# A decoder trunk on one core: the second FFN products of two phases as seven block products, their sums returned through device memory

## The chip, the core and the metric

The kernel runs on one core of a Trainium2 chip. The time is that of one execution on the device in microseconds, as the median of three runs. The engines are named as the profile names them: PE multiplies matrices, PEld loads its weights, DVE and ACT work on elements, POOL starts the software DMAs and does some element work, SP starts the hardware DMAs. All DMA queues of the core use the same 16 DMA engines.

## The reference

Two layers, each a mixer and a feed-forward network (FFN), on x of 512 positions by 1024 in float32. The mixer of layer 0 joins a gated linear recurrence and retention, that of layer 1 is a sparse attention; the change touches neither. The FFN's hidden width is 2816.

```python
def swiglu(x, w1, w3, w2):
    return (jax.nn.silu(x @ w1) * (x @ w3)) @ w2

def reference(x, ...):
    h = x
    for layer in range(DEPTH):
        ...
        h = h + swiglu(rmsnorm(h, ffn_norm[layer]), ffn_w1[layer], ffn_w3[layer], ffn_w2[layer])
    return rmsnorm(h, final_norm)
```

## The kernel before

**Precision.** Every float32 matrix product is made of three matmuls: an operand is split into a high part (`hi`, a copy in a rounded type, ACT, L136 for weights) and what is left (`lo`, a subtraction, DVE, L137), and `mm3` (L201 to L203) adds hi by hi, lo by hi and hi by lo in one PSUM bank.

**Residual stream.** `h` lies transposed in two tiles, feature by position, so a sum that comes out position by feature has to be turned on PE before it can be added.

**Phases.** `ffn` goes through the hidden width in three phases, `ph` 0 and 1 of 1024 and 2 of 768. A phase has two sets (`q` 0 and 1), each of them a call of `strassen`: the products of x with a 512 (384) wide piece of w1 and of w3 in one, as a 2 by 2 block product that takes seven block products instead of eight. These are, in order, A11, A12, S1, S4, S2, S3 and A22, named by their left operand; each is 2 halves of the positions by 4 blocks of the depth by 3 matmuls, 24. They add up in the PSUM banks X, Y, V, V, X, X and Z. Between them `keep` copies a bank away (ACT, L286) and `add` adds a bank to what was kept (DVE, L290), both with the norm's factor for a position. X is used three times over: the kept X of A11, then S2 on top, read for the block 12, then S3 on top, read for the block 22.

**Gating and turning.** `after` (L732) multiplies silu of the one by the other (L741), and `turn` transposes the result on PE (L726) to g, feature by position, in high part `gh` (L729) and low part `gl` (L730).

**Second products.** At the end of each phase g goes through w2 as plain products: 8 tiles of the output, each 8 (6) blocks of depth by 3 matmuls, so 192 for 1024; `done` (L767) adds a tile's PSUM bank to h.

**Weights.** `plan` and `plan_set` list the loads ahead. A plain unit is 1 MB by SP (L117), of two parts of 1024 columns. A set loads three of its four weight blocks by SP and makes the sums that the seven products want in place, by eight accumulating DMAs by POOL (L161): each may only start when DVE has split what stood there. It has 14 parts. Raw weights, high parts and low parts have four buffers each, and splits run three parts ahead of PE. A framework sets the order of each engine from the program's order and priorities; every engine then works in order.

Of the kernel before, what the change touches and what calls it, by code (L numbers as in the profile page):

```python
# [17 lines left out]
F32 = mybir.dt.float32  # L18
F32R = mybir.dt.float32r
# [5 lines left out]
P = 128  # L25
# [38 lines left out]
class Trunk:  # L64
# [210 lines left out]
    def strassen(self, sg, n, after, last):  # L275
# [8 lines left out]
        def keep(b, name, i, r):  # L284
            c = rest[name, i] = self.g2([P, S], name="part")[:, 0:n]
            A.activation(c, ps[b, i][:, 0:n], AF.Copy, scale=r())  # L286

        def add(b, name, i, r):
            c = rest.pop((name, i))
            V.scalar_tensor_tensor(c, ps[b, i][:, 0:n], r(), c, op0=ALU.mult, op1=ALU.add)  # L290
            after(name, i, c)
        R = lambda t: (lambda: self.rtok[:, t:t + 1])
        N = lambda t: (lambda: self.ntok[:, t:t + 1])
        for j, (b, op) in enumerate((("X", "A11"), ("Y", "A12"), ("V", "S1"), ("V", "S4"), ("X", "S2"), ("X", "S3"), ("Z", "A22"))):
            last(j)
            if j == 1:
                for i in range(2):
                    keep("X", "11", i, R(i))
            first = j in (0, 1, 2, 6)
            for i in range(2):  # L300
                if first:
                    ps[b, i] = self.psA("ps_" + b) if b in "XV" else self.psB("ps_" + b)
                o = ps[b, i][:, 0:n]
                self.mm3(o, [self.sg_at(sg, op, p, slice(i * P, (i + 1) * P)) + w.at((j * 4 + p) * n, (j * 4 + p + 1) * n) for p in range(4)], first, True, j in (3, 4, 5))
                if j == 1:
                    add("Y", "11", i, R(i))
                elif j == 2:
                    keep("V", "22", i, R(2 + i))
                elif j == 3:
                    keep("V", "12", i, R(i))  # L310
                elif j == 4:
                    add("X", "12", i, N(i))
                elif j == 5:
                    add("X", "22", i, N(2 + i))
# [369 lines left out]
    def plan_ffn(self, layer):  # L684
        for ph in range(3):
            for j in range(2):
                if ph < 2:
                    self.plan_set("wff%d" % layer, (2 * ph + j,), 2048)
                else:
                    self.plan_set("wfg%d" % layer, (j,), 1536)  # L690
            for j in range(2):
                if ph < 2:
                    self.plan("w2a%d" % layer, 2 * ph + j, 2048)
                else:
                    self.plan("w2b%d" % layer, j, 1536)
            for j in range(2):
                if ph < 2:
                    self.plan("w2c%d" % layer, 2 * ph + j, 2048)
                else:
                    self.plan("w2d%d" % layer, j, 1536, 768)  # L700

    def ffn(self, layer, sg, gain_next, want_hg=True):
# [10 lines left out]

        for ph in range(3):
            gs = []
            for q in range(2):
                n = S if ph < 2 else 3 * P
                nj = n // P
                g = [self.b8([P, 4, S], F32R, name="g" + x) for x in "hl"]
# [3 lines left out]
                def turn(t, v, g=g, nj=nj):  # L723
# [3 lines left out]
                    p4 = pt[:, 0:nj * P].rearrange("p (j c) -> p j c", j=nj)  # L727
                    hi, lo = (x[:, 0:nj, t * P:(t + 1) * P] for x in g)
# [24 lines left out]
                self.strassen(sg, n, after, before)  # L753
# [20 lines left out]
            flush(7)  # L774
            w = [self.unit(), self.unit()]
# [36 lines left out]
        return hn  # L812

# [559 lines left out]
def pack(i):  # L1373
# [28 lines left out]
    for l in range(2):  # L1402
# [8 lines left out]
        o["w2a%d" % l] = c(np.stack([w2u((4 * q, 4 * q + 4), (0, 4)) for q in range(4)]))  # L1411
        o["w2b%d" % l] = c(np.stack([w2u((16 + 3 * q, 19 + 3 * q), (0, 4)) for q in range(2)]))
        o["w2c%d" % l] = c(np.stack([w2u((8 * ph, 8 * ph + 8), (4 + 2 * q, 6 + 2 * q)) for ph in range(2) for q in range(2)]))
# [28 lines left out]
```

## Time and profile before

| | us |
|---|---|
| median of 3 runs | 1243.75 |
| the three runs | 1243.32 to 1243.83 |
| the profiled execution | 1243.25 |
| its span, first to last instruction | 1241.3 |
| PE busy | 1221.3 (98%) |
| DVE busy | 797.6 (64%) |
| ACT busy | 684.3 (55%) |
| POOL busy | 230.8 (19%) |

The span has 1.95 us less than the execution's time. The FFN of layer 0 lies at about 215 to 557 us, that of layer 1 at about 887 to 1235 us. A busy share says how long an engine had work, not whether anybody waited for it; that is seen in waits and in the chain that ended last.

### The profile page before, as it was taken

How to read it: one execution, taken by the hardware profiler on the slowest of the kernel's cores; microseconds unless marked ns; L12 is line 12 of the kernel's file. 1: busy time of each engine (PE TensorE's matmuls, PEld its weight loads, DVE VectorE, ACT ScalarE, POOL GpSimd, SP SyncE). 2: the span in 40 equal slices, each digit the busy share in tenths (PEclk: the TensorE clock that was granted, in tenths of full speed). 3: DMA queues.
4: the chain of work that ended last, by engine and by line, in shares of the span. 5: the costliest groups of instructions: out<-in, count | busy, mean ns of one | idle time of the engine just before them, and what ended most of it. 6: DMA issues, size and time to landing. Idle time of an engine off the chain costs nothing.

```text
span 1241.3 us, 16441 instructions
## 1 busy us (share of the span) xinstructions
PE 1221.3 (98%) x6077; PEld 1030.5 (83%) x6077; DVE 797.6 (64%) x1237; ACT 684.3 (55%) x1395; POOL 230.8 (19%) x303
## 2 busy tenths in 40 slices
PE   9999999999999999999999999999999999999997
PEld 8788888888888889987888878877888888889996
DVE  6886639666356636775264889985976546653664
ACT  6541447664256426655454688995766336633653
POOL 0001420220012002100000567681111011101200
PEclk9999999999999999999999999999999999999999
DMA  9221143784378428852100000124588358825832
GB/s 343 69 102 68 35 169 102 174 187 150 101 182 184 133 69 178 222 201 77 68 35 1 1 1 1 35 96 171 130 182 200 107 124 185 200 81 107 181 90 68
DMA packets 35535, 149.23 MB, mean 120 GB/s; under 512 B 3936, under 2 KB 6256, under 8 KB 26624
## 3 DMA queue, kind: packets, MB, share of 16 engines
q1 hardware_dynamic: 21296, 100.88, 22.7%
q0 software_dynamic: 14016, 47.27, 21.4%
q8 instruction: 48, 0.79, 0.3%
q14 instruction: 31, 0.25, 0.1%
q10 hardware_dynamic: 144, 0.04, 0.0%
HBM read 143.98 MB, written 4.19 MB: 119 GB/s over the span
## 4 chain that ended last, share of the span: by engine, by line
PE 87%; ACT 5%; DVE 4%; issue 1%; POOL 1%; DMA 0%; POOLq 0%; DVEq 0%; SPq 0%; ACTq 0%
PE ps L203 6%; PE ps L201 6%; PE ps L202 6%; PE ps_t L201 5%; PE ps_t L203 5%; PE ps_t L202 5%; PE ps_X L201 5%; PE ps_X L203 5%; PE ps_X L202 5%; PE ps_V L201 3%; PE ps_V L203 3%; PE ps_V L202 3%; ACT prob L1184 2%; PE ps_Y L201 2%; PE ps_Z L201 2%; PE ps_Z L203 2%
## 5 line engine op out<-in xcount | busy, mean ns | idle before, releaser
L136 ACT CAST whi<-wr 128x512 fp32r<-128x512 f32 (+1 forms) x540 | 294.9, 593 | 347.2 <-PE ps L202 126.0
L137 DVE TENSOR_TENSOR wlo<-wr,whi 128x1024 fp32r<-128x1024 f32 (+2 forms) x272 | 313.4, 1154 | 209.1 <-ACT whi L136 201.9
L201 PE MATMUL ps<-gh,whi 128*128 128x512 f32 (+1 forms) x364 | 139.8, 384 | 0.0
L203 PE MATMUL ps<-gh,wlo 128*128 128x512 f32 (+1 forms) x364 | 139.2, 382 | 0.0
L202 PE MATMUL ps<-gl,whi 128*128 128x512 f32 (+1 forms) x364 | 139.1, 382 | 0.0
L161 POOL DMA_DIRECT2D wr<-wff x64 | 55.5, 866 | 376.1 <-DVE wlo L137 329.4
L201 PE MATMUL ps_t<-whi,hgh 128*128 128x512 f32 x288 | 114.7, 399 | 0.0
L202 PE MATMUL ps_t<-wlo,hgh 128*128 128x512 f32 x288 | 113.4, 394 | 0.0
L203 PE MATMUL ps_t<-whi,hgl 128*128 128x512 f32 x288 | 112.7, 391 | 0.0
L201 PE MATMUL ps_X<-whi,sg 128*128 128x512 f32 (+1 forms) x288 | 107.1, 372 | 0.4 <-DVE part L290 0.3
L203 PE MATMUL ps_X<-whi,sg 128*128 128x512 f32 (+1 forms) x288 | 106.9, 371 | 0.0
L202 PE MATMUL ps_X<-wlo,sg 128*128 128x512 f32 (+1 forms) x288 | 106.8, 371 | 0.0
L1194 POOL TENSOR_TENSOR prob<-prob,rs 128x384 f32<-128x384 f32 (+3 forms) x128 | 88.0, 721 | 1.9
L767 DVE TENSOR_TENSOR h<-ps,h 128x512 f32<-128x512 f32 x46 | 31.8, 691 | 82.5 <-PE ps L203 82.5
L203 PEld LDWEIGHTS ps<-gh,wlo 128*128 128x128 f32 x364 | 68.4, 188 | 13.4
L202 PEld LDWEIGHTS ps<-gl,whi 128*128 128x128 f32 x364 | 68.4, 188 | 13.1
L201 PEld LDWEIGHTS ps<-gh,whi 128*128 128x128 f32 x364 | 68.4, 188 | 12.9
L1184 ACT ACTIVATE prob<-ps_s,nm 128x384 f32<-128x384 f32 (+3 forms) x128 | 68.1, 540 | 15.8 <-DVE nm L1180 15.0
L201 PE MATMUL ps_V<-whi,sg 128*128 128x512 f32 (+1 forms) x192 | 71.4, 372 | 0.0
L203 PE MATMUL ps_V<-whi,sg 128*128 128x512 f32 (+1 forms) x192 | 71.2, 371 | 0.0
L202 PE MATMUL ps_V<-wlo,sg 128*128 128x512 f32 (+1 forms) x192 | 71.2, 371 | 0.0
L203 PEld LDWEIGHTS ps_t<-whi,hgl 128*128 128x128 f32 x288 | 54.1, 188 | 11.5 <-issue 0.2
(316 smaller groups left out, 2565.2 us busy)
## 6 DMA issues: line engine op xcount, KB each, us to landing
wr<-wff POOLq DMA_DIRECT2D x64, 512.0 KB, 5.7
wr<-wff SPq DMA_DIRECT2D x24, 1024.0 KB, 4.8
wr<-wfg POOLq DMA_DIRECT2D x32, 384.0 KB, 5.8
wr<-w0t SPq DMA_DIRECT2D x10, 1024.0 KB, 6.0
wr<-w1t SPq DMA_DIRECT2D x10, 1024.0 KB, 4.9
wr<-wfg SPq DMA_DIRECT2D x12, 768.0 KB, 4.4
wr<-w2a SPq DMA_DIRECT2D x8, 1024.0 KB, 4.8
wr<-w2c SPq DMA_DIRECT2D x8, 1024.0 KB, 4.9
```

The costliest lines, as they stand in the source:

```text
L136: self.nc.scalar.copy(hi[:, c], x[:, c])
L137: self.nc.vector.tensor_tensor(lo, x, hi.bitcast(F32), op=ALU.subtract)
L161: self.nc.gpsimd.dma_start(x[:, c], more[:, c], accum_op=ALU.add)
L201: mm(ps, ah, bh, start=(first and k == 0), stop=False)
L202: mm(ps, ah, bl, start=False, stop=False)
L203: mm(ps, al, bh, start=False, stop=(last and k == n - 1))
L767: V.tensor_tensor(hm, ps, hm, op=ALU.add)
L1184: A.activation(u.p[:, r, b, 0:u.nk], u.ps[:, b, :], AF.Exp, bias=u.nm[:, b:b + 1], accum_out=u.rs[:, r, b:b + 1])
L1194: Q.tensor_tensor(x, x, u.rs[:, r, b:b + 1].broadcast_to([P, u.nk]), op=ALU.mult)
```

## The change

In phases 0 and 1 the second products are a `strassen` call too, on new weights `w2s` (three loads and eight accumulations of 512 KB, 14 parts) in place of `w2a` and `w2c` (four plain loads, 8 parts). `second` makes the six operands from g (`make`: ACT high, DVE low, in halves, two operand tiles `gop` in flight) and their sums (`sums1`, `sums2`, DVE). `turn` leaves g as it comes in these phases. The results come out position by feature. They are not added to h but stored in device memory (`sums`, 8 stores a phase by SP). In the last phase, step by step (a step is one block product, 14 in the phase), SP loads the eight tiles of phase 0's sums into the operand buffers of that phase (`back`), POOL adds those of phase 1 to them by accumulating DMAs one step later, and three products behind that `turned` transposes them (4 transposes a tile) and adds them to h. The last phase's own products stay as they were. `keep` and `add` have a form without factor; the sign is in the operation.

```diff
-    def strassen(self, sg, n, after, last):
+    def strassen(self, opnd, n, after, last, scaled=True):
...
+            if scaled:
+                A.activation(c, ps[b, i][:, 0:n], AF.Copy, scale=r())
+            else:
+                with self.tc.high_priority(offset=20):
+                    A.copy(c, ps[b, i][:, 0:n])
...
+                V.tensor_tensor(c, c, ps[b, i][:, 0:n], op=ALU.subtract if sub else ALU.add)
...
+            if ph < 2:
+                self.plan_set("w2s%d" % layer, (ph,), 2048)
+                continue
...
+        sums = self.dram.tile([2, NT, P, D], F32, name="sums%d" % layer)
+        back = []
+
+        def turned(t, c, tiles):
+
+            pt = self.psC("ps_tr")
+            for k in range(4):
+                T.transpose(pt[:, k * P:(k + 1) * P], tiles[:, k * P:(k + 1) * P], self.ident)
+            x = h[c][:, :, t * P:(t + 1) * P]
+            V.tensor_tensor(x, pt.rearrange("p (k s) -> p k s", k=4), x, op=ALU.add)
+
...
+                    if nj == 4:
+                        A.copy(g[:, :, t * P:(t + 1) * P], p4)
+                        return
...
+                    if ph == 2:
+
+                        step = 7 * q + j
+                        for i in range(8):
+                            src = [sums[u, i // 2, :, i % 2 * S:(i % 2 + 1) * S] for u in range(2)]
+                            if step == i + 2:
+                                if i % 4 == 0:
+                                    back.append(self.b8([P, 4, S], name="back"))
+                                nc.sync.dma_start(back[i // 4][:, i % 4], src[0])
+                            elif step == i + 3:
+                                nc.gpsimd.dma_start(back[i // 4][:, i % 4], src[1], accum_op=ALU.add)
+                            elif step == i + 6:
+                                turned(i // 2, i % 2, back[i // 4][:, i % 4])
...
+            if ph < 2:
+                self.second(gs[0][0], gs[1][0], sums[ph], flush)
+                continue
...
+    def second(self, g0, g1, dst, flush):
...
+        def make(n):
+            t = ops[n] = self.b8([P, 2, 4, 256], F32R, name="gop")
+            for c in (slice(0, 2), slice(2, 4)):
+                x = src[n][0 if c.start == 0 else 1] if n == "S1" else src[n][:, c]
+                with self.tc.high_priority(offset=16):
+                    A.copy(t[:, 0, c], x)
+                    V.tensor_tensor(t[:, 1, c], x, t[:, 0, c].bitcast(F32), op=ALU.subtract)
...
+        def before(j):
+            while stores:
+                self.nc.sync.dma_start(*stores.pop(0))
+            if j == 0:
+                make("A12")
+            elif j == 1:
+                flush(99)
+                sums1()
+                make("S1")
+                sums2()
+            elif j < 6:
+                make(("S4", "S2", "S3", "A22")[j - 2])
+
+        def after(name, i, c):
+            t = 2 * (name[0] == "2") + i
+            u = name[1] == "2"
+            stores.append((dst[t, :, u * S:(u + 1) * S], c))
+
+        make("A11")
+        self.strassen(lambda n, p, c: tuple(ops[n][:, z, p, c] for z in range(2)), S, after, before, False)
+        before(7)
```

The order of DVE in the middle of the second product of layer 0's phase 0, before: splits of weights (`wlo`) by turns with adds of a finished bank to h.

```order
L767 TENSOR_TENSOR h_1434<-ps_2_2482,h_1434 128x512
L137 TENSOR_TENSOR wlo_2623<-wr_2384,whi_2622 128x1024
L767 TENSOR_TENSOR h_1435<-ps_2_2621,h_1435 128x512
L137 TENSOR_TENSOR wlo_2656<-wr_2443,whi_2655 128x1024
L767 TENSOR_TENSOR h_1435<-ps_2_2652,h_1435 128x512
L137 TENSOR_TENSOR wlo_2688<-wr_2443,whi_2687 128x1024
```

The same engine at the fifth and sixth product there, after. L866 makes the low part of an operand `gop` (here S3's in the first row and A22's in the fourth), L298 is the new `add`; banks `ps_X_2482` and `ps_X_2508` are the two halves of X.

```order
L866 TENSOR_TENSOR gop_2685<-g_1814,gop_2685 128x512 x2
L137 TENSOR_TENSOR wlo_2691<-wr_2337,whi_2690 128x1024
L298 TENSOR_TENSOR part_2669<-part_2669,ps_X_2482 128x512
L866 TENSOR_TENSOR gop_2730<-g_2155,gop_2730 128x512 x2
L137 TENSOR_TENSOR wlo_2698<-wr_2062,whi_2697 128x1024
L137 TENSOR_TENSOR wlo_2736<-wr_2062,whi_2735 128x1024
L298 TENSOR_TENSOR part_2683<-part_2683,ps_X_2508 128x512
L298 TENSOR_TENSOR part_2624<-part_2624,ps_X_2482 128x512
```

The second add of a pair (its bank is `ps_X_2508`) now has the making of an operand and two splits between it and the first.

PE in the second product there, before: one bank after the other, each from g.

```order
L203 MATMUL ps_2_2479<-gh_1813,wlo_2387 128x512
L201 MATMUL ps_2_2480<-gh_1813,whi_2386 128x512
L202 MATMUL ps_2_2480<-gl_1814,whi_2386 128x512
L203 MATMUL ps_2_2480<-gh_1813,wlo_2387 128x512
L201 MATMUL ps_2_2480<-gh_1813,whi_2386 128x512
```

PE at the sixth product, after: twelve matmuls into `ps_X_2482`, the last two of which are the first rows here, three of the seventh product (`ps_Z_2780`), then twelve into `ps_X_2508`.

```order
L202 MATMUL ps_X_2482<-wlo_2691,gop_2685 128x512
L203 MATMUL ps_X_2482<-whi_2690,gop_2685 128x512
L201 MATMUL ps_Z_2780<-whi_2697,gop_2730 128x512
L202 MATMUL ps_Z_2780<-wlo_2698,gop_2730 128x512
L203 MATMUL ps_Z_2780<-whi_2697,gop_2730 128x512
L201 MATMUL ps_X_2508<-whi_2652,gop_2685 128x512
L202 MATMUL ps_X_2508<-wlo_2653,gop_2685 128x512
```

The sixth product adds to banks that the adds of the fences above read, and three matmuls of the seventh stand between its halves.

POOL in the last phase of layer 0, before: the sixteen accumulations of weights for the two sets.

```order
L161 DMA wr_3343<-wfg0 128x768 x4
L161 DMA wr_3488<-wfg0 128x768 x2
L161 DMA wr_3343<-wfg0 128x768 x2
L161 DMA wr_3553<-wfg0 128x768 x4
L161 DMA wr_3820<-wfg0 128x768 x2
L161 DMA wr_3553<-wfg0 128x768 x2
```

The same, after; `back` are the returning sums.

```order
L782 DMA back_3875<-sums0_1813 128x512 x2
L161 DMA wr_3350<-wfg0 128x768 x2
L782 DMA back_3875<-sums0_1813 128x512 x2
L782 DMA back_4058<-sums0_1813 128x512 x3
L161 DMA wr_3350<-wfg0 128x768 x2
L782 DMA back_4058<-sums0_1813 128x512
L161 DMA wr_3666<-wfg0 128x768 x2
L161 DMA wr_3350<-wfg0 128x768 x2
```

Two returns stand ahead of the first pair of weights, five between the first pair and the second, and one between the second and the third.

## Rows read from the trace of the kernel before

**Rows 1.** The page: busy time by engine, clock by slice, chain that ended last.
```profile
PE 1221.3 (98%) x6077; PEld 1030.5 (83%) x6077; DVE 797.6 (64%) x1237; ACT 684.3 (55%) x1395; POOL 230.8 (19%) x303
...
PEclk9999999999999999999999999999999999999999
...
PE 87%; ACT 5%; DVE 4%; issue 1%; POOL 1%; DMA 0%; POOLq 0%; DVEq 0%; SPq 0%; ACTq 0%
```

**Rows 2.** By stage: busy time of each engine; its line of titles comes first.
```profile
core 0: us, PE busy (x) PEld busy (x) DVE busy (x) ACT busy (x) POOL busy (x), PEclk, DMA share, GB/s
295.10:339.60 44.50, 44.50 (x202) 36.89 (x202) 18.43 (x21) 10.32 (x20) 1.72 (x2) 1.00 0.37 106
339.60:378.60 39.00, 39.00 (x178) 32.40 (x177) 24.45 (x26) 24.10 (x42) 6.92 (x8) 1.00 0.75 175
378.60:418.50 39.90, 39.90 (x186) 33.19 (x185) 27.37 (x31) 25.11 (x44) 5.17 (x6) 1.00 0.78 185
418.50:462.90 44.40, 44.40 (x201) 36.84 (x200) 17.55 (x21) 9.60 (x19) 1.73 (x2) 1.00 0.28 77
462.90:493.30 30.40, 30.13 (x176) 29.68 (x174) 19.14 (x26) 19.33 (x42) 6.91 (x8) 1.00 0.74 163
493.30:523.80 30.50, 30.50 (x181) 30.32 (x181) 21.02 (x31) 20.23 (x45) 5.74 (x7) 1.00 0.89 204
```

**Rows 3.** Waits of 295 to 557 us on PE, of 460 to 527 on ACT.
```profile
engine line waited for: us in total, times, longest us
PE ps_X L201 <- DVE part L290: 0.3, 1, 0.3
...
ACT whi L136 <- DMA wr<-wfg: 3.8, 5, 1.2
```

**Rows 4.** Timeline of PE: start, duration, operation; one product's first matmul and transposes.
```profile
303.08 0.40 PE L203 MATMUL ps<-gh,wlo 128*128 128x512 f32 x1
303.31 1.04 PE L726 MATMUL ps_tr<-ident,part 128*128 128x128 f32 x8
304.11 0.47 PE L201 MATMUL ps<-gh,whi 128*128 128x512 f32 x1
304.42 0.39 PE L202 MATMUL ps<-gl,whi 128*128 128x512 f32 x1
...
350.47 0.39 PE L201 MATMUL ps_V<-whi,sg 128*128 128x512 f32 x1
...
361.35 0.39 PE L201 MATMUL ps_X<-whi,sg 128*128 128x512 f32 x1
```

**Rows 5.** Timeline of PE, ACT and DVE near a set's fourth to sixth products.
```profile
401.03 0.39 PE L203 MATMUL ps_V<-whi,sg 128*128 128x512 f32 x1
401.25 0.39 PE L201 MATMUL ps_X<-whi,sg 128*128 128x512 f32 x1
...
401.45 1.15 ACT L136 CAST whi<-wr 128x512 fp32r<-128x512 f32 x2 [0.22 <-PE ps_V L203]
402.50 0.68 ACT L286 ACTIVATE part<-ps_V,rtok 128x512 f32<-128x512 f32 x1
...
406.75 1.22 DVE L137 TENSOR_TENSOR wlo<-wr,whi 128x1024 fp32r<-128x1024 f32 x1 [0.43 <-ACT whi L136]
407.89 0.74 DVE L290 SCALAR_TENSOR_TENSOR part<-ps_X,ntok,part 128x512 f32<-128x512 f32 x1
```

**Rows 6.** Groups by shape over the span: count, busy us, mean ns of one.
```profile
L137 DVE TENSOR_TENSOR wlo<-wr,whi 128x1024 fp32r<-128x1024 f32 x204 | 249.5, 1225 | 162.5 <-ACT whi L136 159.8 <-PE ps_t L203 0.3
...
L767 DVE TENSOR_TENSOR h<-ps,h 128x512 f32<-128x512 f32 x46 | 31.8, 691 | 82.5 <-PE ps L203 82.5
```

**Rows 7.** The page's DMA queues and issues (KB each, us from issue to landing).
```profile
q1 hardware_dynamic: 21296, 100.88, 22.7%
q0 software_dynamic: 14016, 47.27, 21.4%
...
wr<-wfg POOLq DMA_DIRECT2D x32, 384.0 KB, 5.8
...
h<-hdram SPq DMA_DIRECT2D x8, 256.0 KB, 4.4
```

**Rows 8.** A stretch of the last phase with accumulating DMAs alone, columns as in rows 2.
```profile
501.00:514.00 13.00, 13.00 (x77) 12.89 (x76) 7.29 (x9) 8.08 (x17) 3.63 (x5) 1.00 1.03 171
```

**Rows 9.** Timeline of POOL in the last phase's first set.
```profile
468.47 0.86 POOL L161 DMA_DIRECT2D wr<-wfg  x1 [13.38 <-DVE wlo L137]
469.51 0.86 POOL L161 DMA_DIRECT2D wr<-wfg  x1 [0.18 <-issue]
472.63 0.86 POOL L161 DMA_DIRECT2D wr<-wfg  x1 [2.25 <-DVE wlo L137]
474.03 0.86 POOL L161 DMA_DIRECT2D wr<-wfg  x1 [0.53 <-DVE wlo L137]
```

More of the change, by code (lines that the diff above doesn't have):

```diff
@@ L303, in strassen @@
                 o = ps[b, i][:, 0:n]
-                self.mm3(o, [self.sg_at(sg, op, p, slice(i * P, (i + 1) * P)) + w.at((j * 4 + p) * n, (j * 4 + p + 1) * n) for p in range(4)], first, True, j in (3, 4, 5))
+                self.mm3(o, [opnd(op, p, slice(i * P, (i + 1) * P)) + w.at((j * 4 + p) * n, (j * 4 + p + 1) * n) for p in range(4)], first, True, j in (3, 4, 5))
                 if j == 1:
@@ L311, in strassen @@
                 elif j == 4:
-                    add("X", "12", i, N(i))
+                    add("X", "12", i, N(i), True)
                 elif j == 5:
-                    add("X", "22", i, N(2 + i))
+                    add("X", "22", i, N(2 + i), True)
                     keep("X", "21", i, R(2 + i))
@@ L718, in ffn @@
                 nj = n // P
-                g = [self.b8([P, 4, S], F32R, name="g" + x) for x in "hl"]
+                g = [] if ph == 2 else self.b8([P, 4, S], name="g")
                 gs.append((g, nj))
@@ L727, in turn @@
                     p4 = pt[:, 0:nj * P].rearrange("p (j c) -> p j c", j=nj)
+                    if nj == 4:
+                        A.copy(g[:, :, t * P:(t + 1) * P], p4)
+                        return
+                    if not g:
+                        g[:] = [self.b8([P, 4, S], F32R, name="g" + x) for x in "hl"]
                     hi, lo = (x[:, 0:nj, t * P:(t + 1) * P] for x in g)
@@ L752, in ffn @@
                 later[:] = [(j - 7, f) for j, f in later]
-                self.strassen(sg, n, after, before)
+                self.strassen(partial(self.sg_at, sg), n, after, before)
             if ph == 2 and want_hg:
@@ L812, in ffn, with sums1, sums2 @@
         return hn
+    def second(self, g0, g1, dst, flush):
+        V, A = self.nc.vector, self.nc.scalar
+        a, b = slice(0, 256), slice(256, S)
+        src = {"A11": g0[:, :, a], "A12": g1[:, :, a], "S3": g0[:, :, b], "A22": g1[:, :, b], "S2": g0[:, :, a], "S4": g1[:, :, a]}
+        ops = {}
+        def make(n):
[5 more added lines that the diff above has]
+                    V.tensor_tensor(t[:, 1, c], x, t[:, 0, c].bitcast(F32), op=ALU.subtract)
+        def sums1():
+            src["S1"] = []
+            for c in (slice(0, 2), slice(2, 4)):
+                x = self.g2([P, 2, 256], name="s1")
+                V.tensor_tensor(x, g0[:, c, b], g1[:, c, b], op=ALU.subtract)
+                src["S1"].append(x)
+        def sums2():
+            for z, c in enumerate((slice(0, 2), slice(2, 4))):
+                V.tensor_tensor(g0[:, c, b], g0[:, c, a], g0[:, c, b], op=ALU.subtract)
+                V.tensor_tensor(g0[:, c, a], src["S1"][z], g0[:, c, a], op=ALU.subtract)
+                V.tensor_tensor(g1[:, c, a], g1[:, c, a], g0[:, c, a], op=ALU.add)
+        stores = []
+        def before(j):
[17 more added lines that the diff above has]
+        before(7)
     def rope(self, x, n, cos, sin):
```

21 lines of the change are left out of this document (8 added, 13 removed).

## The prediction

> **What bounds the kernel now.** I read the page's first sections, then a table of the first layer's FFN by stage, then the timelines of each engine in the stages that the change touches, then queues and waits. The first group is to show that TensorE (PE) is busy for 98% of the span, makes up 87% of the chain that ended last, and has the full granted clock in every slice [rows 1]. The table by stage says where the change falls: the second products take 44.50 and 44.40 us with PE busy throughout, beside sets of 39.00 and 39.90 us (1024 hidden) and of 30.40 and 30.50 us (768 hidden) [rows 2]. In the second products DVE is busy for 18.43 of 44.50 us and the DMA share is 0.37; in the last phase's sets it is 0.74 and 0.89. Between 295 and 557 us PE waited for one thing, once, for 0.3 us [rows 3]. So a matmul saved on PE is time saved, in full, and every other engine and the transfers have to stay behind PE for that to stay true. That is the question of this case: what was off the path by how much.
>
> **The change part by part.** Times are of the profiled execution, 1243.25 us for a span of 1241.3; the median of the three runs is 0.5 us higher, which I leave out.
>
> *Matmuls taken away.* Four second products (two phases, two layers) go from 192 matmuls to 7 x 24 = 168. The pitch is 48 starts in 361.35 - 350.47 = 10.88 us, 0.227 us each [rows 4]. 4 x 24 x 0.227 = **-21.8 us**, all on the path.
>
> *Transposes added.* The sums of two phases now come back in the third, 8 tiles a layer of 4 transposes each. A pair of such groups took 304.11 - 303.31 = 0.80 us, and the matmul after it took 0.31 until the next start where 0.227 is usual [rows 4]: 0.88 a pair, 0.44 a group. 16 groups are **+7.1 us**. The transposes of g are as many as before.
>
> *The wait at X12.* In a set the fifth and sixth products (S2, S3) accumulate in the same bank X, and between them DVE must read it (the adds named X12). The order of the changed kernel puts, behind the first of the two adds, the making of operand A22 (two subtractions) and two splits of weights, and only then the second add; PE, in order, has three matmuls of A22 and then the sixth product's second half, which waits for that add. It is so in all four second products; in the first sets one split stands there. What DVE does there is timed by ACT, which has to make each high part first. A22's buffer is the one that S2 leaves, so nothing of it starts before S2's last matmul is through, T. ACT takes over 0.20 us later (the last matmul of V's slot ends at 401.25, the cast starts at 401.45), and has two casts for A22 and four for the two weight parts: two casts start 402.50 - 401.45 = 1.05 us ahead of the next operation [rows 5], so six need 3.15 and the last one's end 0.1 more, T + 3.45. DVE's last split starts then, the add stands 1.14 us behind it (406.75 to 407.89) [rows 5] and lasts 0.69, as the adds from a PSUM bank do [rows 6], and 0.1 to 0.2 us go to the hand-over: T + 5.4. PE has half a product (2.72 us by the pitch) and three matmuls (0.68) to do, so it stands from T + 3.4 for 2.0 us. If ACT is further ahead than I think the wait is 1.3; with every split and add at its full mean (1.225, 0.691) [rows 6] and no overlap 3.2. I take 2.05: 4 x 2.05 = **+8.2 us** (5.2 to 12.8). The rows show an operation's end and the next one's start to overlap: a split of 1.22 us is followed after 1.14 [rows 5]. The Trainium skill (VectorE: DVE Perf Modes, "The DRAIN you can't avoid") says that the next operation does not start until the pipe is empty; the wait would be 2.6 us a time by that, 10.4 in all, and the rows here disagree.
>
> *DVE and ACT in the second products.* DVE gets 14 splits (1.14 us pitch), 14 half makings, 8 sums and 8 adds (0.6 to 0.66): 16.0 + 19.0 = 35 us in about 41, where it had 18.43 busy [rows 2, 6]. ACT gets 28 casts for weights, 14 for operands, 6 copies: 48 x 0.55 = 26 us. Both fit, DVE narrowly. The operand S4 passes through the sums, and by the same counting is ready some 0.3 us before PE wants it. I give such places 0.2 us a second product, **+0.8** (0 to 4). The turn of g loses its eight subtractions a set on DVE, and its casts stay: that hides, being off the path in a stage where DVE had room.
>
> *The returns.* Sixteen stores of 256 KB leave by SP, eight loads come back by SP and eight accumulating DMAs by POOL a layer, in the last phase's fourteen products. Elsewhere the transfers have room: a second product's weights are now three loads of 1 MB and eight accumulations of 512 KB, as in a first set, where the share is 0.75 to 0.78 [rows 2], and eight stores. In the last phase the prices come from rates: 100.88 MB took 22.7% of the span in the hardware queue, so 358 GB/s of all engines, and 47.27 MB took 21.4% in the software queue, 178 GB/s [rows 7]; where only accumulations run the share is 1.03 at 171 GB/s [rows 8]. So 2.1 MB back costs 5.9 us, 2.1 MB accumulated 11.8, the stores of a phase 5.9. The first set of the phase has 0.74 x 30.4 = 22.5 us of transfers already. To it come six loads (4.4), five accumulations (7.4) and the last four stores (2.9): 37 us in 30.4. The second set gets 2 loads and 3 accumulations: 27 + 5.9 = 33 in 30.5. The queue decides the same: POOL has two accumulations of weights at 468.47 and 469.51 and the next two at 472.63 and 474.03 [rows 9]; five returns now stand between these, 5 x 0.86 us of issue and 7.4 us of transfer in the same queue. A weight part is wanted three parts ahead of PE, 3 x 2.2 = 6.5 us, and ACT already waited for such a transfer five times, 3.8 us in all [rows 3], so some 4 to 5 us are truly free. Of a backlog of 9 I leave 4.5 us to PE, a layer: **+9.0 us** in two. Bounds: 0 (all of it is hidden, POOL idles for 13 us ahead of the first of them, [rows 9]) and 26, twice the 13 us of new work (7.4 + 5.9) if none hides.
>
> *Hidden edits.* The eight adds into h of a phase go from the second products to eight a layer in the last phase, on DVE, which has 11 and 9 us free in those sets [rows 2]; if that cover failed each is 0.69 us. The transposes stand three products (12.5 us) behind their transfer, so PE waits for the sums themselves only if one lands later than that; a load takes 4.4 us from issue [rows 7].
>
> *Sum.* -21.8 + 7.1 + 8.2 + 0.8 + 9.0 = +3.3; 1243.25 + 3.3 = **1246.5 us**.
>
> **The rivals.** *A, the forecast*: half the gain goes to X12 and transposes, the rest to crowded transfers. With the ends that I hold likely (X12 6 to 10, transfers 6 to 15) it runs from 1241 to 1254.
>
> *B, transfers have room.* POOL is mostly idle and its accumulations are released by DVE's splits [rows 9], and the shares of a set are below 0.9 [rows 2]; if the queues interleave so that weights lose no more than their slack, the 9.0 become 1: 1238.5, faster by 5 us. Against it: the two queues' shares together reach 1 in some stretches [rows 8], and five returns stand ahead of weights.
>
> *C, slower: the returns hold the weights.* Place: the first set of the last phase, B22's accumulation behind five returns. Price: with no slack left, because the second product before it (ph 1) now also fills its queue, 9 to 13 us of backlog reach PE in each layer: -21.8 + 7.1 + 8.2 + 0.8 + 18 to 26 = +12 to +20, 1256 to 1264. It decides once free slack falls under about 1 us. For it: POOL's queue is in order and the software queue alone reaches 1.03 [rows 8]. The Trainium skill (DMA: Bandwidth & Descriptors, on queue rows that share the sixteen engines) has the engines take the queue rows in turn, packet by packet. Rows 7 and 8 agree in that the shares add up. By that rule each queue's weights slow as the other gets busy, which is this rival's price and no gain.
>
> *D, DVE becomes the bound.* 35 of 41 us by pitch leaves little; if the operands are late at S1, S4 and S2 by 1 us each, as ACT and DVE hand each one over in turn, each second product loses 3 us more: +12, 1258. Against it: operands stand at raised priority.
>
> *E, it doesn't do what it says*: the count of matmuls is in the order of the changed kernel, so this has no chance of its own.
>
> **How the numbers follow.** A 0.45, B 0.27, C 0.18, D 0.10. A measurement of this kernel tells about 0.2%, 2.5 us, from no change: faster is below 1241.3, slower above 1246.2. A lies around the upper line: 0.03 faster, 0.18 the same, 0.24 slower. B is faster at 0.25, the same at 0.02. C and D are slower, 0.28. Together 0.28, 0.20 and 0.52. The range leaves out most of C's end, and the low end of B: 1237 to 1259. The likeliest case's own range is 1241 to 1254.
>
> **What would show it.** In the changed kernel each second product should take about 41 us with 168 matmuls at 0.227, PE should wait on X12's add once in each of the four for about 2 us, and the transposes should take 0.4 to 0.5 us a group. In the last phase's first set the transfer share should be near 1, ACT should wait for accumulations of weights, and PE for the low parts, 4 to 5 us a layer. If the sets stay at 30.4 us plus their transposes, it is B; if they grow past 40, C; waits on operands in second products are D. The forecast is wrong if PE waits for something that isn't listed, above all for the sums themselves, or if the matmuls of the new products have another pitch.

## The result and the profile after

The changed kernel takes 1264.26 us (median of 4 runs, 1263.13 to 1264.48) where the kernel before takes 1243.79 on the same chip: a ratio of 1.0158, 95% interval 1.0143 to 1.0173. It is slower by 20.5 us; forecast were 1246.5 us and a range to 1259. The profiled span is 1261.4 us, 20.1 more than before.

The page of the changed kernel, its parts on busy time, clock by slice, transfers by slice and DMA queues:

```profile
PE 1215.7 (96%) x6045; PEld 1024.0 (81%) x6045; DVE 865.1 (69%) x1333; ACT 756.1 (60%) x1531; POOL 272.6 (22%) x351
...
PEclk9999999999999998999999999999999999998998
DMA  8121144787988798852110000133678897799732
...
q0 software_dynamic: 20928, 68.25, 29.9%
q1 hardware_dynamic: 27632, 109.27, 24.5%
```

PE works 5.6 us less than in [rows 1], and the span is 20.1 us longer: PE now stands still. The clock row has a lower figure in the slices of two pauses of 9.4 us, one in each layer (that of layer 0 is shown below), and in the last. The software queue has gone from 47.27 to 68.25 MB [rows 7].

The same stages as in [rows 2], after (columns as there), the first set of the last phase cut at the start and the end of PE's trouble (463.49 and 484.71), and the list of PE's waits over the span:

```profile
295.30:335.66 40.36, 39.31 (x178) 32.30 (x176) 34.28 (x44) 27.21 (x50) 6.90 (x8) 1.00 0.87 209
...
414.53:455.14 40.61, 39.32 (x177) 32.31 (x176) 34.05 (x45) 26.59 (x50) 8.66 (x10) 1.00 0.88 209
455.14:463.49 8.35, 8.35 (x50) 8.34 (x48) 3.15 (x4) 2.44 (x5) 1.72 (x2) 1.00 1.09 257
463.49:484.71 21.22, 10.82 (x49) 10.02 (x49) 6.47 (x9) 7.35 (x16) 8.80 (x10) 0.78 1.09 247
```

```profile
PE ps_V L201 <- ACT part L288: 18.8, 2, 9.4
PE ps_X L201 <- DVE part L298: 5.5, 4, 1.9
...
PE ps_V L202 <- DVE wlo L137: 1.0, 1, 1.0
```

The second products of layer 0 take 40.4 and 40.6 us instead of 44.5 and 44.4. What they give is lost, and more, in one place a layer: two products (S1 and S4, bank V) of the last phase's first set take 21.22 us where 48 matmuls of 384 columns need 8.3, with the transfer share above 1. PE stands there for 9.4 us in each layer. The list names ACT, the last of what the matmul waited for; what ACT and DVE waited for comes below.

For all kernels of this study the same reading, from PE's timeline, the first matmul of a stage to the first of the next. The four second products are added up; "set 1" and "set 2" are those of the last phase, in layer 0 and layer 1. The stages are of the profiled execution, the medians of all; the profiled executions of e5, e8 and e10 were 3.6, 1.9 and 3.4 us faster than their medians, that of e6 2.2 us slower.

| kernel | median us | four second products | set 1 | set 2 |
|---|---|---|---|---|
| before | 1243.8 | 177.7 | 30.4, 29.8 | 30.5, 30.9 |
| after | 1264.3 | 164.3 | 44.2, 43.0 | 33.5, 33.4 |
| e1 no wait for the stores | 1263.1 | 164.2 | 45.5, 41.2 | 33.5, 33.5 |
| e2 nothing returns | 1230.7 | 165.0 | 30.4, 30.7 | 30.9, 30.4 |
| e3 returns behind weights | 1256.1 | 164.6 | 35.3, 33.3 | 38.4, 38.9 |
| e4 X12 first | 1260.7 | 158.9 | 44.1, 44.8 | 33.5, 33.5 |
| e5 an eighth accumulated | 1255.1 | 164.7 | 38.6, 36.6 | 33.5, 33.5 |
| e6 added by DVE | 1254.9 | 164.3 | 39.9, 39.1 | 34.1, 34.5 |
| e7 no trip, X12 first | 1236.8 | 167.4 | 30.8, 31.2 | 30.7, 30.8 |
| e8 returns late | 1251.4 | 162.7 | 31.7, 30.9 | 39.2, 39.0 |
| e9 e8 and X12 first | 1245.7 | 158.9 | 31.9, 31.4 | 40.0, 39.3 |
| e10 e3 and e5 | 1243.9 | 164.2 | 33.5, 31.7 | 33.5, 33.5 |
| e11 e2 and X12 first | 1224.6 | 158.9 | 30.7, 30.5 | 30.8, 30.4 |
| e12 returns a phase earlier | 1237.5 | 169.0 | 30.8, 31.2 | 30.7, 30.7 |

Set 1 and set 2 of the changed kernel hold two and six groups of returned transposes. One of them alone takes 0.35 us and makes the matmul after it 0.09 later (a product of 24 matmuls takes 4.25 behind it, where 4.16 is usual), so 0.44: 0.9 and 2.6 us of the two sets. That leaves 13.0 and 12.3 us lost in set 1 and nothing in set 2.

### The profile page after: what moved, and what is told of

It is laid out like the page before. It is cut to its first block, busy times and chain, and to the rows that moved or that the text cites. A ratio compares the mean times of both kernels' runs of the same rounds, so it can differ in the third digit from the quotient of the medians.

```text
span 1261.4 us, 16868 instructions
## 1 busy us (share of the span) xinstructions
PE 1215.7 (96%) x6045; PEld 1024.0 (81%) x6045; DVE 865.1 (69%) x1333; ACT 756.1 (60%) x1531; POOL 272.6 (22%) x351
## 3 DMA queue, kind: packets, MB, share of 16 engines
q0 software_dynamic: 20928, 68.25, 29.9%
## 5 line engine op out<-in xcount | busy, mean ns | idle before, releaser
L137 DVE TENSOR_TENSOR wlo<-wr,whi 128x1024 fp32r<-128x1024 f32 (+1 forms) x296 | 342.5, 1159 | 235.1 <-ACT whi L136 225.1
L136 ACT CAST whi<-wr 128x512 fp32r<-128x512 f32 (+1 forms) x588 | 322.8, 596 | 282.2 <-PE ps_t L203 51.3
L201 PE MATMUL ps_V<-whi,sg 128*128 128x512 f32 (+1 forms) x192 | 73.7, 384 | 18.9 <-ACT part L288 18.8
L203 PE MATMUL ps_V<-whi,sg 128*128 128x512 f32 (+1 forms) x192 | 72.8, 379 | 0.0
L201 PEld LDWEIGHTS ps_t<-whi,hgh 128*128 128x128 f32 x288 | 54.2, 188 | 11.5 <-ACT tok_v L523 0.6
L202 PEld LDWEIGHTS ps_t<-wlo,hgh 128*128 128x128 f32 x288 | 54.2, 188 | 10.6 <-issue 0.5
L1273 DVE TENSOR_REDUCE nm<-ps_s 128x1 f32<-128x384 f32 (+3 forms) x96 | 56.8, 595 | 7.3 <-PE ps_s L1269 6.3
L201 PEld LDWEIGHTS ps_X<-whi,sg 128*128 128x128 f32 x288 | 54.7, 190 | 8.3 <-DVE part L296 0.4
L202 PEld LDWEIGHTS ps_X<-wlo,sg 128*128 128x128 f32 x288 | 54.6, 190 | 7.5
L203 PEld LDWEIGHTS ps_X<-whi,sg 128*128 128x128 f32 x288 | 54.5, 189 | 7.5
L1299 DVE TENSOR_TENSOR ptl<-ps_tr,pth 128x512 fp32r<-128x512 f32 x80 | 54.2, 680 | 6.3 <-ACT pth L1296 5.1
```

What stands on the lines that cost most here:

```text
L136: self.nc.scalar.copy(hi[:, c], x[:, c])
L137: self.nc.vector.tensor_tensor(lo, x, hi.bitcast(F32), op=ALU.subtract)
L201: mm(ps, ah, bh, start=(first and k == 0), stop=False)
L202: mm(ps, ah, bl, start=False, stop=False)
L203: mm(ps, al, bh, start=False, stop=(last and k == n - 1))
L1273: V.tensor_reduce(u.nm[:, 0:u.n], u.ps, axis=AX.X, op=ALU.max, negate=True)
```

## Where the time goes in set 1

PE's timeline at the pause of layer 0, and ACT's behind it:

```profile
470.94 0.34 PE L203 MATMUL ps_V<-whi,sg 128*128 128x384 f32 x1
480.71 0.69 PE L201 MATMUL ps_V<-whi,sg 128*128 128x384 f32 x1 [9.43 <-ACT part L288]
481.19 0.52 PE L202 MATMUL ps_V<-wlo,sg 128*128 128x384 f32 x1
481.51 0.52 PE L203 MATMUL ps_V<-whi,sg 128*128 128x384 f32 x1
...
467.15 0.58 ACT L288 ACTIVATE part<-ps_V,rtok 128x384 f32<-128x384 f32 x1
477.36 0.92 ACT L136 CAST whi<-wr 128x384 fp32r<-128x384 f32 x2 [9.62 <-DMA wr<-wfg]
479.25 0.92 ACT L136 CAST whi<-wr 128x384 fp32r<-128x384 f32 x2 [0.97 <-DMA wr<-wfg]
480.08 1.04 ACT L288 ACTIVATE part<-ps_V,rtok 128x384 f32<-128x384 f32 x2
```

ACT waited 9.62 us for an accumulated weight part. PE does not need that part yet: the pause stands ahead of the second half of S4, whose own weights were split, and the late part is one of S2's. PE waits for the `keep` that reads the second half of bank V (L288 at 480.08; that of the first half is at 467.15), and this `keep` stands in ACT's queue behind the four casts of the late weights. So the 12 matmuls of that half, 2.1 us, had to wait as well; an order with the `keep` first was not tried. After the pause the matmuls start 0.32 us apart in place of 0.173. The table by stretch gives the granted clock as 0.50 there, the lower of the two levels, 1.2 GHz:

```profile
480.80:485.60 4.80, 4.80 (x15) 4.80 (x16) 1.33 (x2) 1.90 (x5) 0.86 (x1) 0.50 1.08 205
486.00:493.00 7.00, 7.00 (x42) 7.00 (x41) 5.39 (x8) 3.43 (x8) 0.00 (x0) 1.00 0.52 142
```

So of the 13.0 us of layer 0 a pause is 9.4, a wait for a low part ahead of it 1.0, and the slow clock behind it some 2.2 (15 matmuls x 0.147). POOL's timeline shows where the weight part was, in the changed kernel and then in e2, the kernel without returns:

```profile
448.17 1.75 POOL L782 DMA_DIRECT2D back<-sums  x2 [9.79 <-issue]
451.42 0.86 POOL L161 DMA_DIRECT2D wr<-wfg  x1 [1.49 <-DVE wlo L137]
452.88 0.86 POOL L161 DMA_DIRECT2D wr<-wfg  x1 [0.60 <-DVE wlo L137]
456.30 0.86 POOL L782 DMA_DIRECT2D back<-sums  x1 [2.56 <-DMA back<-sums]
461.58 0.86 POOL L782 DMA_DIRECT2D back<-sums  x1 [4.42 <-issue]
466.00 1.75 POOL L782 DMA_DIRECT2D back<-sums  x2 [3.56 <-DMA sums<-part]
469.57 0.86 POOL L782 DMA_DIRECT2D back<-sums  x1 [1.81 <-DMA sums<-part]
470.10 2.11 POOL L161 DMA_DIRECT2D wr<-wfg  x2
```

```profile
460.83 0.86 POOL L161 DMA_DIRECT2D wr<-wfg  x1 [7.28 <-DVE wlo L137]
461.89 0.86 POOL L161 DMA_DIRECT2D wr<-wfg  x1 [0.20 <-issue]
```

Set 1 starts at 455.14 after and at 454.94 in e2. The second pair of weights is issued 15.0 us into the set after and 5.9 us in e2: 9.1 us late, the length of the pause. In between POOL is not busy issuing: it stands with five returns, each of which waits for something of its own to land. The notes in the rows name a load once, a store twice and nothing once, but the landings in the trace are plainer: the loads of the five land at 455.8, 461.1, 465.5, 466.4 and 468.3 and the last store at 469.0. Each return starts 0.5 us behind its own load, only the fifth behind the store. The Trainium skill (TensorE: Matmul & The Clock Gate, under "Architectural detail", on engine queue depths) calls GpSimd's queue a strict first-in, first-out one; POOL's rows agree, the weights did not overtake.

Not all of the 9.1 us is that order. The first pair of weights, behind two returns, took 9.9 and 11.0 us to land, where e2's took 5.8 and 6.9, so DVE had it split only at 463.6 and 465.9; from there the returns held the second pair for about 6 and 4.5 us.

Why loads and weights take long to land is the second half. The list of issues of the changed kernel (KB each, us to landing):

```profile
sums<-part SPq DMA_DIRECT2D x32, 256.0 KB, 6.1
back<-sums SPq DMA_DIRECT2D x16, 256.0 KB, 9.7
back<-sums POOLq DMA_DIRECT2D x16, 256.0 KB, 7.4
```

A load of 256 KB took 4.4 us before [rows 7] and takes 9.7 here. Over 446 to 486 us the DMA share is 1.06 on average, where the stretch of the kernel before that answers to it, 453 to 493, has 0.62 (first after, then before):

```profile
446.00:486.00 40.00, 28.31 (x135) 25.96 (x135) 15.27 (x20) 14.79 (x32) 14.01 (x16) 0.87 1.06 255
```

```profile
453.00:493.00 40.00, 39.73 (x218) 37.59 (x217) 21.42 (x29) 19.98 (x44) 7.77 (x9) 1.00 0.62 133
```

So two causes offer themselves: POOL's order, and the bytes. The experiments take them apart.

## Experiments on the returns

**e1, no wait for the stores.** The first theory was that POOL stands for the last stores of phase 1, as two of its rows say.

```diff
-src = [sums[u, i // 2, :, i % 2 * S:(i % 2 + 1) * S] for u in range(2)]
+src = [sums[0, i // 2, :, i % 2 * S:(i % 2 + 1) * S] for u in range(2)]
```

> The returning accumulations read phase 0's sums a second time in place of phase 1's (so phase 1's share is left out of the result). POOL's order, all bytes and all queues stay; only the wait for the stores of the second product of phase 1 is gone. Theory W (POOL, in order, stands for the landing of the last stores, and the weights' accumulations stand behind it): the wait of 9.4 us at ps_V shrinks to 4 us or less in each layer, 1244 to 1251 us. Theory T (there are too many bytes in the last phase's first set, whatever waits for what): the wait stays at 8 us or more, 1260 us or more.

Measured 1263.05 us (ratio 1.0146, 1.0131 to 1.0161), no better. PE's waits, and POOL's timeline ahead of the weights:

```profile
PE ps_V L201 <- ACT part L288: 19.1, 3, 9.7
```

```profile
459.45 0.86 POOL L782 DMA_DIRECT2D back<-sums  x1 [4.92 <-issue]
464.22 0.86 POOL L782 DMA_DIRECT2D back<-sums  x1 [3.91 <-DMA back<-sums]
468.38 2.75 POOL L782 DMA_DIRECT2D back<-sums  x3 [3.30 <-issue]
470.82 2.10 POOL L161 DMA_DIRECT2D wr<-wfg  x2
```

The wait for the stores is gone and POOL stands as long for the loads of the returns: they land at 458.9, 463.7, 467.9, 468.5 and 469.8, and each of the five returns starts 0.5 us behind its own. That theory falls: only the fifth return had waited for a store, which landed 0.7 us behind its load.

**e2, nothing returns.** The loop over returns is left empty.

```diff
-                        for i in range(8):
+                        for i in range(0):
```

> No sums come back: the eight loads, eight accumulations, transposes and adds of each layer's last phase are left out (so two phases' share is left out of the result); the stores stay. Both theories: no wait at ps_V in the last phase, so 2 x 12.5 us of stall with its slow matmuls and 7.1 us of transposes less, 1230 to 1234 us. If a wait of over 4 us stays there, the weights or the stores alone are too much, and the returns aren't the cause.

Measured 1230.71 us (0.9887, 0.9872 to 0.9902), as expected. Set 1 is as before the change, with the stores and the denser weights still there. The returns cost 33.5 us in all, of which 7.1 are transposes on PE.

**e3, returns behind the weights.** The numbers of steps in the program do not order POOL's queue: the first return belongs to the fourth product of set 1, and POOL issued it at 448.17, before the set's first matmul. So the accumulation was tied to a weight part of the later products, by an operation on one column that changes nothing.

```diff
...
-                            elif step == i + 3:
+                            elif step == 4 + i // 3:
+                                x = back[i // 4][:, i % 4, 0:1]
+                                V.scalar_tensor_tensor(x, self.ready[-1][1][:, 0:1].bitcast(F32), 0.0, x, op0=ALU.mult, op1=ALU.add)
                                 nc.gpsimd.dma_start(back[i // 4][:, i % 4], src[1], accum_op=ALU.add)
```

(The loads are issued from step 2 + i // 3 on.)

> The same returns, the accumulations held back by an operation on one column that needs a weight part of the fifth to seventh product of the set, so that POOL takes them up behind the set's accumulations of weights; transposes where they were. Theory W: PE waits 1 us or less at ps_V, 1237 to 1242 us. Theory T: the same bytes in the same 30 us, PE still waits 5 us or more a layer, 1253 us or more.

Measured 1256.10 us (1.0089, 1.0069 to 1.0108), in the second expectation by the time; PE's wait at ps_V, 4.6 us in both layers together, lies between the two. PE's waits:

```profile
...
PE ps_tr L727 <- DVE gl L753: 4.7, 2, 2.4
PE ps_V L201 <- ACT part L288: 4.6, 3, 2.6
PE ps_tr L744 <- DVE h L729: 3.6, 2, 2.3
```

The wait at ps_V went from 18.8 to 4.6 us, set 1 got shorter by 9.0 and 9.7 us. Set 2 got 4.9 and 5.4 us longer. The added operation is not the reason: e10 has it too, and its set 2 is as in the changed kernel. The hold came back there (POOL, ACT and DVE of layer 0):

```profile
488.50 2.46 POOL L161 DMA_DIRECT2D wr<-wfg  x1
502.75 0.92 ACT L136 CAST whi<-wr 128x384 fp32r<-128x384 f32 x2 [5.45 <-DMA wr<-wfg]
503.70 0.96 DVE L137 TENSOR_TENSOR wlo<-wr,whi 128x768 fp32r<-128x768 f32 x1 [4.82 <-ACT whi L136]
```

A weight part of set 2 was issued at 488.50, behind all eight returns, and landed 14.1 us later. ACT's cast waits for it, DVE's split waits for the cast, and gl and h, for which PE waits, stand in DVE's queue behind such splits.

**e5, an eighth of the accumulated bytes.** Order and number of DMAs as in the changed kernel.

```diff
-nc.gpsimd.dma_start(back[i // 4][:, i % 4], src[1], accum_op=ALU.add)
+nc.gpsimd.dma_start(back[i // 4][:, i % 4, 0:64], src[1][:, 0:64], accum_op=ALU.add)
```

> The returning accumulations add 64 of 512 columns (the other columns of phase 1's sums are left out of the result): 7/8 of their bytes go, some 10 us of the software queue a layer; POOL's order, its issues and what it waits for stay. Theory T (bytes): PE waits 4 us or less at ps_V in each layer, 1240 to 1250 us. Theory O (POOL stands in order for the loads of the returns, however little is added): the wait stays at 8 us or more, 1258 us or more.

Measured 1255.09 us (1.0090, 1.0073 to 1.0107); the wait at ps_V is 9.6 us, in two. Between the two expectations: set 1 got shorter by 5.7 and 6.4 us.

**e10, the edits of e3 and e5 together.**

> POOL's order as in e3, and 64 of 512 columns accumulated as in e5 (the rest of phase 1's sums is left out of the result). e3 took away the order and e5 most of the bytes; each left about 4 to 8 us of stall in the first set of the last phase. If order and bytes are the two causes, together they leave 1 to 3 us a layer: 1240 to 1247 us. If a third cause (SP's loads of weights behind its stores) holds the rest, the stall stays near 4 us a layer: 1249 us or more.

Measured 1243.88 us (0.9990, 0.9979 to 1.0001), as expected of two causes, and

```profile
PE ps_V L201 <- ACT part L288: 3.0, 2, 2.4
```

The four kernels make a square. Lost in set 1 beyond the 0.9 us of transposes, in us, layer 0 and layer 1:

| | all bytes accumulated | an eighth |
|---|---|---|
| POOL's order as changed | 13.0, 12.3 | 7.3, 5.9 |
| weights first | 4.0, 2.6 | 2.2, 1.0 |

Order and bytes are both causes. In set 1 the order is the larger: it alone takes away about 9 of 13, the bytes alone 6 in the profiled executions. Over the phase it is not: with weights first and all bytes set 2 loses 5.2 and 5.4 us beyond its transposes, in the other three 0.3 at most. By the medians e3 saves 8.2 us, e5 9.2 and e10 20.4. The two work through one another, since a return that lands later holds the weights behind it longer. The last 1 to 2 us are gone in e2, which has the stores; whether the loads or what is left of the accumulations hold them was not tried.

**e6, returns by SP alone.** Both phases' sums are loaded and DVE adds them.

```diff
...
-                                nc.sync.dma_start(back[i // 4][:, i % 4], src[0])
-                            elif step == i + 3:
-                                nc.gpsimd.dma_start(back[i // 4][:, i % 4], src[1], accum_op=ALU.add)
...
+                                for u in range(2):
+                                    nc.sync.dma_start(back[u][:, i % 4], src[u])
+                            elif step == i + 5:
+                                V.tensor_tensor(back[0][:, i % 4], back[0][:, i % 4], back[1][:, i % 4], op=ALU.add)
...
```

> No accumulating return: SP loads both phases' sums (sixteen loads a layer) and DVE adds them, one product before the transposes. POOL has only weights to do, so nothing stands ahead of them. Theory O: no wait at ps_V, 1237 to 1243 us. Theory T: the bytes stay, at the hardware queue's price (5.9 us in place of 11.8): PE still waits 3 to 6 us a layer, 1246 to 1256 us.

Measured 1254.91 us (1.0088, 1.0073 to 1.0103), with 10.7 us of waits at ps_V. POOL has weights alone, and set 1 still loses 8.6 and 8.4 us. But this run does not take the hold away, it moves it to DVE (DVE, then POOL, layer 0):

```profile
463.14 0.69 DVE L783 TENSOR_TENSOR back<-back 128x512 f32<-128x512 f32 x1 [3.60 <-DMA back<-sums]
463.75 1.82 DVE L137 TENSOR_TENSOR wlo<-wr,whi 128x768 fp32r<-128x768 f32 x2
464.99 1.76 POOL L161 DMA_DIRECT2D wr<-wfg  x2 [11.60 <-DVE wlo L137]
```

DVE's add of a return waits 3.60 us for a load, and behind it stands the split of a weight part whose casts were done at 459.8. So POOL could issue the second pair of weights only 10.2 us into the set, where e2 has 5.9. The transfers slow one another too: the first two pairs took 6.7 to 8.5 us to land, in e2 5.0 to 6.9. The Trainium skill's rule from the prediction (DMA: Bandwidth & Descriptors, queue rows served in turn) fits this: weights in one queue slowed as the other filled.

**e8, everything late.** The loads as well are tied to a weight part, from step 3 on, and the transposes stand in steps 8 to 13.

```diff
-                            if step == i + 2:
+                            if step == 3 + i // 2:
...
+                                x = back[i // 4][:, i % 4, 0:1]
+                                V.tensor_copy(x, self.ready[-1][1][:, 0:1].bitcast(F32))
                                 nc.sync.dma_start(back[i // 4][:, i % 4], src[0])
-                            elif step == i + 3:
+                            elif step == 4 + i // 2:
...
-                            elif step == i + 6:
+                            if step == 8 + (2 * i + 1) // 3:
```

> All returns, loads and accumulations, start later: each load overwrites a column that a weight part of the set's later products had to be written to first; POOL has all eight accumulations of the set's weights ahead of them. Transposes in steps 8 to 13. If the two causes are the order on POOL and the crowd of transfers in the set's first 15 us, and not the sum of bytes over the phase, PE waits 1 us or less at ps_V and nothing new comes: 1237 to 1242 us. If the phase as a whole is too full, the waits move to the second set: 1247 us or more.

Measured 1251.39 us (1.0055, 1.0039 to 1.0071). Set 1 is nearly clean (31.7 and 30.9), and set 2 takes 39.2 and 39.0: with all eight groups of transposes there (3.5 us), 5.2 and 4.6 us are lost. PE's waits in set 2 of layer 0:

```profile
PE ps_tr L744 <- DVE h L729: 2.4, 1, 2.4
PE ps_V L201 <- ACT part L288: 2.2, 1, 2.2
```

The loss moved and shrank, from 12.6 to about 6 us a layer: the bytes are not free in set 2 either, placed like this.

**e9, the edits of e8 and of e4 (X12's second add first, below).**

> The run before with X12's second add ahead of the splits as well: another 3 to 6 us less than it, 1232 to 1238 us if that gives 1237 to 1242.

Measured 1245.74 us (1.0009, 1.0000 to 1.0018): 5.7 us less than e8, as expected of X12, and no gain over the kernel before.

## Experiments on X12

**e4, X12's second add ahead of the splits.** The unscaled `add` gets a raised priority.

```diff
-                V.tensor_tensor(c, c, ps[b, i][:, 0:n], op=ALU.subtract if sub else ALU.add)
+                with self.tc.high_priority(offset=40):
+                    V.tensor_tensor(c, c, ps[b, i][:, 0:n], op=ALU.subtract if sub else ALU.add)
```

> The returns as in the changed kernel; the adds of the second products have a higher priority, so that X12's second add stands ahead of the two splits. If the wait at X12 is DVE's order alone, the four waits (5.5 us by the list of waits, 6.1 by the starts, and slower matmuls behind the last) go: 1255 to 1259 us. If DVE is full there, the splits come later in turn and PE waits for low parts instead: 1262 to 1265 us.

Measured 1260.73 us (1.0134, 1.0112 to 1.0156), 3.5 us less, between the two expectations. The second products give 5.4 us in the table, and set 1 of layer 1 takes 1.8 of them back (43.0 to 44.8). It may be that the stall there ends with a transfer, so that who comes earlier waits longer; layer 0 does not show it (44.2 to 44.1).

**e11, the same without returns: the edits of e2 and e4.**

> e2 (nothing comes back; two phases' share left out of the result) with X12's second add ahead of the splits. If X12's wait is DVE's order alone: the 6 us of four waits go, 1223 to 1226 us. If DVE's splits are then late instead, as some were in e4 (3.4 us of waits for low parts): 1227 to 1230 us.

Measured 1224.56 us (0.9837, 0.9820 to 0.9853), 6.15 us less than e2. Where no transfer sets the end, the full price of X12's order comes back, and DVE keeps up with the splits. In the last second product of layer 1 the wait had a sequel, in the changed kernel too: PE's granted clock was 0.50 behind a pause of 1.89 us (timeline of the changed kernel, then the table by stretch),

```profile
1129.55 0.50 PE L201 MATMUL ps_X<-whi,gop 128*128 128x512 f32 x1 [1.89 <-DVE part L298]
```

```profile
1131.30:1134.30 3.00, 3.00 (x9) 2.33 (x8) 1.27 (x2) 1.18 (x3) 1.58 (x3) 0.50 0.93 300
```

which makes that product 42.8 us in place of 40.5. By the starts, PE lost 2.05 us in that pause; in the other three it lost 1.2 to 1.45 and the clock held.

## Versions that beat both

**e7, no trip through memory.** Each block of a second product is transposed where it is, two products later, and added to h: 32 groups of transposes instead of 16, and no store, load or return (with the edits of e2 and e4).

```diff
+            now[0] = j
+            flush(j)
...
-            stores.append((dst[t, :, u * S:(u + 1) * S], c))
+            later.append((now[0] + 2, partial(turned, t, int(u), c)))
```

> No trip through device memory: each sum of a second product is transposed from where it was made, two products later, and added to h; 32 groups of transposes in place of 16; X12's second add ahead of the splits as in the run before. Both theories: no wait in the last phase; -21.8 + 14.1 + about 1 against the kernel before, 1236 to 1240 us. If DVE, which gets eight more adds in each second product, is full there: PE waits for adds or low parts, 1245 us or more.

Measured 1236.82 us (0.9940, 0.9925 to 0.9955): faster than both kernels. By the terms of the prediction, -21.8 for matmuls and 32 x 0.44 = 14.1 for transposes make -7.7; measured are -7.2. DVE is busy for 37.30 of 41.87 us in such a second product, and PE does not wait for it:

```profile
294.90:336.77 41.87, 41.87 (x202) 34.69 (x200) 37.30 (x49) 27.79 (x52) 6.92 (x8) 1.00 0.79 176
```

**e12, returns a phase earlier.** Phase 0's sums come back in the second product of phase 1, POOL adds them to the new block, and 16 groups of transposes do (with the edits of e2 and e4).

```diff
+            if ph == 1:
+                for t, u in {0: ((0, 0), (1, 0)), 3: ((0, 1), (1, 1)), 4: ((2, 1), (3, 1)), 5: ((2, 0), (3, 0))}.get(j, ()):
+                    got[t, u] = self.g2([P, S], name="got")
+                    self.nc.sync.dma_start(got[t, u], dst[t, :, u * S:(u + 1) * S])
...
+            self.nc.gpsimd.tensor_tensor(c, c, got.pop((t, int(u))), op=ALU.add)
```

> Phase 0's sums are stored as in the changed kernel, but come back in the second product of phase 1 (eight loads by SP, where the changed kernel has eight stores), are added there by POOL to the block just made, and each block is transposed two products later and added to h. 16 groups of transposes, no accumulating return, nothing extra in the last phase; X12's second add ahead of the splits. If the last phase's crowd was the trouble and POOL's adds (0.7 us each for 384 columns elsewhere in the kernel) find room between its accumulations of weights: 7.1 us of transposes more than e11 at most, 1229 to 1233 us. If POOL's adds hold up the weights' accumulations behind them: 1236 us or more.

Measured 1237.47 us (0.9947, 0.9930 to 0.9963), level with e7 and 5 us above what was hoped. Set 1 and set 2 are clean. The second product of phase 1 takes 44.1 and 45.6 us, where 39.7 and the six of its eight groups that fall into it make 42.3. PE waits for low parts of operands there, 1.6 us a layer, in layer 1 with slow matmuls behind it. One of POOL's adds costs 1.83 us. The 0.7 of the expectation is a mean over four shapes; POOL's products of this shape, 128x512, take 1.04 in the attention (PE's waits, then the group by shape):

```profile
PE ps_V L203 <- DVE gop L867: 3.1, 2, 1.6
```

```profile
L913 POOL TENSOR_TENSOR part<-part,got 128x512 f32<-128x512 f32 x16 | 29.2, 1831 | 19.1 <-DVE part L299 19.1
```

Whether POOL's adds make DVE late there, or the order does, was not tried.

## Why the prediction was wrong, by its steps

- **Matmuls taken away, -21.8 us: right.** 168 a second product, at 0.227 us. e7 confirms the sum of this and the next term within 0.5 us.
- **Transposes, 0.44 us a group, +7.1: right**, 0.35 + 0.09 in the changed kernel.
- **X12, +8.2, and operands, +0.8: right in kind, nearly in size.** A second product without any wait would be 168 x 0.2267 and 0.88 for the pair of g's transposes in it, 38.97 us; the four took 1.4, 1.6, 1.5 and 3.8 more, 8.4 together, where 9.0 was forecast. The split is another one: PE stood some 1.2 to 1.5 us for X12 in three of them, below the 2.05 taken, the fourth paid for a slow clock as well, and S4 cost nothing. Rival D, late operands, did not come. The section of the Trainium skill that this step sets against the rows (VectorE: DVE Perf Modes, "The DRAIN you can't avoid") goes on to say that an operation that is not held starts earlier, so the rows, in which operations start earlier, do not disagree with it.
- **Returns, +9.0: this step failed.** It measured 25.3 (13.0 and 12.3, set 2 adding nothing); with it and the 8.4 the sum is -21.8 + 7.1 + 8.4 + 25.3 = +19.0, against 20.1 of the spans. The place was named (the first set of the last phase, the weights behind five returns) and so was the backlog, 9 us. The failing sentence is that "some 4 to 5 us are truly free", which left 4.5 to PE. It compared sums of transfer time with the room in a set. Not in it were these: a return in POOL's queue holds the weights until its own load or store has landed, and not only for its own transfer; in a full stretch a load takes 9.7 us and not 4.4, and the first weights 9.9 and 11.0; and the second product before the set has a transfer share of 0.88 where it had 0.28 (e2 shows that this costs nothing without the returns). PE did not stand for low parts, as was forecast, but for 1.0 us: it stood for a bank whose `keep` ACT had behind the late casts. The slow clock after the pause added 2.2 us more. What each of these is worth by itself was not measured, beyond the square of four kernels.
- **Rival C was the case.** Its place and mechanism are those of the rows; it gave 1256 to 1264 with 18 to 26 us for the returns, and they cost 25. That the number comes so near is in part luck: C priced the backlog of transfers alone, and the 13.0 us hold a slow clock of 2.2 that it did not have. Its chance, 0.18, was too small. Its own condition could have been read from rows at hand: 13 us of new work, 22.5 us of old, and a second product ahead that goes from a share of 0.28 to that of a first set.
- **Rival B, transfers have room, fell**; e2, without the returns, shows that weights and stores alone had it. What the prediction held against B, two queues' shares that reach 1 together, is not what its row shows: in [rows 8] one queue is alone.
- That the adds into h would hide on DVE held in the changed kernel, where PE never waited for them.

## What to carry to other kernels

Ask of every DMA that is put into an engine's queue what it waits for, and not only what it moves: a return that waits for its load holds everything behind it, on POOL in the changed kernel and on DVE in e6. Follow what a repair gives back behind it: the weights first saved 9 of 13 us in their set and lost 5 in the next, seven eighths of the accumulated bytes saved about 6, and only both together 11 a layer. Sum the transfers by stretch, the one ahead included. And price the detour by doing the work in place: 16 more groups of transposes (7 us) were cheaper than the trip through memory that saved them.

## What was not expected of the hardware

A pause of 1.89 us on PE was followed by about 3 us at the granted clock of 0.50, in one of four such places; in the others PE lost 0.6 to 0.8 us less and the clock held; after 9.4 us it was 4.8 us. In e12 a pause of 1.56 us stands in both layers, and the matmuls behind it are slow only in layer 1. POOL's addition of 128 x 512 took 1.83 us on average beside a busy DVE (41.1 of 44.05 us), where its products of the same shape in another stage took 1.04 (L1194 before, mean of 32); whether DVE is the reason was not tried. And 256 KB from device memory took 9.7 us from issue to landing in a full stretch, 4.4 elsewhere.
